# One layer of a gated hybrid encoder: the first norm with tokens on partitions and TensorE transposes, and the memory's norm behind u

## The chip, the core and the metric

The kernel runs on one core of one Trainium2 chip. The core has five engines with queues of their own: TensorE (PE; its weight loads are listed apart as PEld), VectorE (DVE), ScalarE (ACT), GpSimd (POOL) and SyncE (SP), which here only issues DMAs. The metric is the time of one execution in device microseconds. One execution was also recorded by the hardware profiler; its trace and the page made from it are what the prediction reads.

## The reference

The layer works on a residual stream x of 512 tokens by 1024 channels and on 256 memory tokens of the same width, in float32. Cut to what this case touches:

```python
def rmsnorm(x, g):
    r = lax.rsqrt(jnp.mean(xf * xf, axis=-1, keepdims=True) + EPS)
    return (xf * r).astype(x.dtype) * g
...
u = rmsnorm(h, g_mix[l])
proj = u @ w_in[l]            # q, k, v of two attentions, gates, decay columns
...
mkv = rmsnorm(mem, g_mem[l]) @ w_mem_kv[l]
mk, mv = jnp.split(mkv, 2, axis=-1)
```

All that follows hangs on u: a gated linear attention, a forgetting attention ("fox"), an attention into the memory, a gated merge with an output projection, an MLP and a last norm.

## The kernel before

**Products.** Each float32 product is made of three matmuls on numbers that are split into a high and a low part: hi x hi, hi x lo and lo x hi (`mm3`, lines 123 to 125). Weights come in chunks of 128 x 1024 floats (512 KB). For each, ScalarE casts the high part and VectorE subtracts it from the original for the low part (`split_w`, lines 115 and 116; `split`, lines 175 and 176; `lead`, lines 255 and 256, for the first five chunks, which are loaded ahead). `gT` multiplies one chunk of weights (as the stationary operand) with activations that have channels on partitions, 24 matmuls for a chunk. `gN` multiplies four chunks (as the moving operand) with blocks of 128 tokens.

**Order.** TensorE executes its instructions in the order in which the program states them (the manual schedule in `build`). The order on the other engines is made by a scheduler of the language from estimated times; `tc.issue_after` holds instructions back behind a given one. Each engine works through its queue in order.

**The front** (lines 239 to 348) comes first. The memory is loaded with channels on partitions (`memr`), scaled by its gain and split (`mxh`, `mxl`). Because the scale of a token factors out of a product, its norm is not needed for the product itself: the four k projections of the memory (`mk_proj`, chunks 0 to 3 of `w_mem_kv`, 24 matmuls of 256 columns each) and its v projection (`mv`, four more chunks, 48 matmuls of 512 columns) run on the unnormalised memory. ScalarE squares the memory, GpSimd adds the eight squares (`sq_cols`, lines 178 to 188), four one-column matmuls against a column of ones sum over the partitions (`rms_cols`, line 196), VectorE and GpSimd form the power -1/2 (`rsqrt`, lines 202 and 203), and `bcast_rows` (lines 211 to 213) makes from it a diagonal matrix whose product with ones is the scale as a row on all partitions (`rmb`). The v projection is scaled by `rm` when it leaves PSUM.

x is loaded with channels on partitions as well (`xr`). Its squares are added on VectorE and GpSimd, summed by 16 one-column matmuls, spread to rows by four products (`rxb`), and each of the eight slices of 128 channels becomes u by a multiplication with gain and scale (line 339; line 337 on GpSimd for two slices) and is split into `uhi` and `ulo`. TensorE's program is: k projections 0 and 1, the memory's column sums, k projection 2, the memory's broadcast, k projection 3, the v projection with x's column sums behind its second step of three matmuls and x's broadcast behind its seventh.

**Behind the front** TensorE does the G chunk (24 matmuls, the first users of u), the first pair of fox projections fq and fk (`fox_pair(0)`), the decay logs, and then everything else. `mem_split` (behind u by `issue_after`) finishes the memory's k and v: `mk_evac` multiplies each k projection by `rmb` and splits it, and the v projection is split.

Of the kernel before, what the change touches and what calls it, by code (L numbers as in the profile page):

```python
# [17 lines left out]
P = 128  # L18
# [40 lines left out]


@with_exitstack
def hybrid_block(ctx, tc, chunks, wst, xT, memT, xN, cols, gffn, gfin, wup, cst, out):
    nc = tc.nc
    PSUM = bass.MemoryType.PSUM
    index = {c: i for i, c in enumerate(chunks)}
# [3 lines left out]
    def nm(s):  # L69
        uid[0] += 1  # L70
        return f"{s}_{uid[0]}"
# [13 lines left out]
    def at_(shape=None):  # L85
        return pa.tile(shape or [P, 512], F32, tag="a", name=nm("a"))
# [84 lines left out]
    def of(hi, lo):  # L171
        return lambda k, sl: (hi[:, k, sl], lo[:, k, sl])

    def split(hi, lo, src):
        nc.scalar.copy(hi, src)  # L175
        return nc.vector.tensor_tensor(lo, src, f(hi), op=ALU.subtract).ins  # L176

    def sq_cols(pool_, src, n, k, accs, pool_ks, tag):

        e = 1 if k in pool_ks else 0  # L180
        eng = nc.gpsimd if e else nc.vector
        if accs[e] is None:
            accs[e] = pool_.tile([P, n], F32, tag=f"{tag}_acc{e}", name=nm("acc"))
            nc.scalar.activation(accs[e], src[:, k, :], AF.Square)
        else:
            sq = pool_.tile([P, n], F32, tag=f"{tag}_sq{e}", name=nm("sq"), bufs=2)
            nc.scalar.activation(sq, src[:, k, :], AF.Square)
            eng.tensor_tensor(accs[e], accs[e], sq, op=ALU.add)

    def rms_cols(pool_, accs, n):  # L190

        accs = [a for a in accs if a is not None]
        ps = at_()
        for t in range(n // P):
            for i, a in enumerate(accs):
                nc.tensor.matmul(ps[:, t:t + 1], a[:, t * P:(t + 1) * P], ones[:, 0:1], start=i == 0, stop=i == len(accs) - 1)
        return rsqrt(pool_, ps[:, :n // P], 1.0 / D, n // P)

    def rsqrt(pool_, ss, inv, n):
        ms = pool_.tile([P, n], F32, tag="ms", name=nm("ms"), bufs=2)  # L200
        r = pool_.tile([P, n], F32, tag="rr", name=nm("rr"), bufs=2)
        nc.vector.tensor_scalar(ms, ss, inv, EPS, op0=ALU.mult, op1=ALU.add)
        nc.gpsimd.tensor_tensor(r, ms, mhalf[:, :n], op=ALU.pow)
        return r

    def bcast_rows(pool_, r, n, rb):

        ps = at_()
        for t in range(n // P):
            dg = pool_.tile([P, P], F32, tag="dg", name=nm("dg"), bufs=2)  # L210
            nc.scalar.mul(dg, ident, r[:, t:t + 1])
            nc.tensor.matmul(ps[:, t * P:(t + 1) * P], ones, dg, start=True, stop=True)
        nc.scalar.copy(rb, ps[:, :n])
# [24 lines left out]

    with pool("front") as fp:
        rmb = gv[:, 0, 0:M]  # L240
        rxb = fp.tile([P, S], F32, name="rxb")
        memr = fp.tile([P, KT, M], F32, name="memr")
        xr = fp.tile([P, KT, S], F32, name="xr")
        pre = {}

        def lead(key, n, i):
            if key not in pre:
                late = index[key] > 2
                pre[key] = [(fp if late else wp).tile([P, 1024], F32, tag="lead" if late else "raw", name=nm("raw"),
                                                      bufs=2 if late else 3)]  # L250
                pre[key] += [wp.tile([P, 1024], F32R, tag=g, name=nm(g)) for g in ("hi", "lo")]
            sl = slice(i * 1024 // n, (i + 1) * 1024 // n)
            raw, hi, lo = (t[:, sl] for t in pre[key])
            nc.sync.dma_start(raw, wst[index[key]][:, sl])
            nc.scalar.copy(hi, raw)
            nc.vector.tensor_tensor(lo, raw, f(hi), op=ALU.subtract)

        mxh = fp.tile([P, KT, M], F32R, name="mxh")
        mxl = fp.tile([P, KT, M], F32R, name="mxl")
        warm = fp.tile([P, 1], F32, name="warm")  # L260
        nc.vector.memset(warm, 0.0)
        wz = fp.tile([P, 512], BF16, name="wz")
        nc.gpsimd.memset(wz, 0.0)
        ps = at_()
        for _ in range(12):
            nc.tensor.matmul(ps, wz[:, :P], wz, start=True, stop=True)
        nc.scalar.activation(warm, warm, AF.Exp)
        nc.sync.dma_start(cols_s, cols)
        macc, xacc = [None, None], [None, None]
        for j in range(4):  # L270
            nc.sync.dma_start(memr[:, 2 * j:2 * j + 2], memT[:, 2 * j:2 * j + 2])
            for k in (2 * j, 2 * j + 1):
                nc.scalar.mul(mxh[:, k, :], memr[:, k, :], gmem[:, k:k + 1])
                nc.vector.scalar_tensor_tensor(mxl[:, k, :], memr[:, k, :], gmem[:, k:k + 1], f(mxh[:, k, :]),
                                               op0=ALU.mult, op1=ALU.subtract)
                if k == 2 * j:
                    lead(chunks[0], 4, j)
        lead(chunks[1], 1, 0)
        nc.sync.dma_start(cst_s[:, :2 * P], cst[:, :2 * P])
        nc.sync.dma_start(cst_s[:, 6 * P:], cst[:, 6 * P:])  # L280
        lead(chunks[2], 1, 0)
        for j in range(4):
            nc.sync.dma_start(xr[:, 2 * j:2 * j + 2], xT[:, 2 * j:2 * j + 2])
            if j == 1:
                lead(chunks[3], 1, 0)
        lead(chunks[4], 1, 0)
        nc.sync.dma_start(cst_s[:, 2 * P:6 * P], cst[:, 2 * P:6 * P])
        nc.sync.dma_start(wup_s, wup)
        for k in range(KT):
            sq_cols(fp, memr, M, k, macc, range(KT), "m")  # L290

        get_plain = get_w

        def get_first(key):
            return pre[key][1:] if key in pre else get_plain(key)

        get_w = get_first
        UP = (2, 5)

        def mk_evac(h):  # L300
            raw = mk_raw(h)
            nc.vector.tensor_tensor(raw, raw, rmb, op=ALU.mult)
            split(mkh[:, h, :], mkl[:, h, :], raw)

        def mk_raw(h):
            return gkT[h // 2][:, (h % 2) * M:(h % 2) * M + M]

        def mk_proj(h):
            run(gT(("T", "w_mem_kv", P * h), mxh, mxl, lambda ps: nc.scalar.copy(mk_raw(h), ps[:, :M]), n=M))
            for k in (2 * h, 2 * h + 1):  # L310
                sq_cols(fp, xr, S, k, xacc, (1, 2, 3), "x")
                if k in UP:
                    nc.scalar.mul(xr[:, k, :], xr[:, k, :], gmix[:, k:k + 1])

        def mv_evac(t, ps):
            nc.scalar.mul(gqT[t], ps, rm[:, t:t + 1])

        mk_proj(0)
        mk_proj(1)
        rm = rms_cols(fp, macc, M)  # L320
        mk_proj(2)
        bcast_rows(fp, rm, M, rmb)
        mk_proj(3)
        nc.vector.tensor_copy(ident16, ident)
        nc.vector.tensor_scalar(cmask, tri, -1.0, -NEG, op0=ALU.add, op1=ALU.mult)
        nc.vector.tensor_copy(msk_s.rearrange("p a b -> p (a b)"), cst_s[:, 4 * P:6 * P])
        mv = gN([("N", "w_mem_kv", 2 * j, 512) for j in range(4)], of(mxh, mxl), 2, mmt, mv_evac)
        for _ in range(2):
            next(mv)
        rx = rms_cols(fp, xacc, S)  # L330
        for _ in range(5):
            next(mv)
        bcast_rows(fp, rx, S, rxb)
        for k in range(KT):
            ut = fp.tile([P, S], F32, tag="ut", name=nm("ut"), bufs=3)
            if k in UP:
                nc.gpsimd.tensor_tensor(ut, xr[:, k, :], rxb, op=ALU.mult)
            else:
                nc.vector.scalar_tensor_tensor(ut, xr[:, k, :], gmix[:, k:k + 1], rxb, op0=ALU.mult, op1=ALU.mult)
            u_end = split(uhi[:, k, :], ulo[:, k, :], ut)  # L340
        run(mv)
        get_w = get_plain

        def mem_split():
            for h in range(4):
                mk_evac(h)
            for t in range(2):
                split(mvh[:, t, :], mvl[:, t, :], gqT[t])


    with pool("fox") as xp:
# [6 lines left out]
            return gT(("T", "w_in", c), uhi, ulo, evac)  # L358

        run(gT(("G",), uhi, ulo, ga_evac))  # L360
        lf = xp.tile([P, NT, 8], F32, name="lf")
        ab = xp.tile([P, NT, 264], F32, name="ab")
        Fc = xp.tile([P, NT, 8], F32, name="Fc")
# [638 lines left out]
def layout(inputs):  # L1002
# [25 lines left out]
    def tl(a):  # L1028
# [20 lines left out]
    cst[:, 5 * P:6 * P] = same & (s > t)  # L1049
    cst[:, 6 * P:6 * P + 8] = -0.5  # L1050
    arrays = {
        "wst": wst, "xT": tl(x), "memT": tl(mem), "xN": np.ascontiguousarray(x), "cols": cols,
        "gffn": np.ascontiguousarray(np.broadcast_to(np.asarray(inputs["g_ffn"])[0], (P, D))),
        "gfin": np.ascontiguousarray(np.broadcast_to(np.asarray(inputs["g_final"]), (P, D))),
        "wup": wup, "cst": cst,
# [24 lines left out]
```

## Time and profile before

| what | value |
|---|---|
| time, median of 3 runs | 864.08 us (863.69 to 866.55) |
| the profiled execution, its own time | 865.53 us |
| its span in the trace | 863.7 us, mean granted TensorE clock 0.992 |
| busy time of PE / PEld | 847.6 us (98%) / 700.0 us (81%) |
| busy time of DVE / ACT / POOL | 493.8 us (57%) / 403.4 us (47%) / 88.3 us (10%) |
| DMA | 106.10 MB, mean 123 GB/s |

The span runs from the first to the last recorded instruction; the execution's own time is 1.8 us longer. Busy shares are means over the whole span. In rows of single instructions the first number is the start in us from the start of the span, the second the duration, then engine, line, operation, output and inputs, and in brackets the idle time ahead of it with the instruction that ended it; "x24" behind a row says that it stands for 24 instructions of that kind. A wait row gives the summed idle time, its count and its longest. A row of stretches gives a time window, its length, the busy time (and count) of PE, PEld, DVE, ACT and POOL, the clock that TensorE was granted (1.00 is full speed), the mean busy share of the DMA engines and GB/s.

### The profile page before, as it was taken

Reading aid. Unit: us, or ns where it says so; the run is one execution under the profiler, and the core shown is the slowest. Engines: PE = TensorE matmul, PEld = TensorE weight load, DVE = VectorE, ACT = ScalarE, POOL = GpSimd, SP = SyncE. Lnnn points to the kernel's source line nnn. Section 1 sums busy time; section 2 is a strip of 40 time slices with the busy share of each in tenths; the row PEclk is TensorE's granted clock in tenths of the full one; section 3 lists DMA queues with packets and bytes.
Section 4 is the critical chain, followed back from the end, with each engine's and each line's share of the span. In section 5 each row is a group of like instructions: output and inputs, shape, how many; then the busy total and the mean of one; then the engine's idle time right before and its main releaser. Section 6 shows DMA issues by size and latency. Waiting matters only on the chain.

```text
span 863.7 us, 10684 instructions
## 1 busy us (share of the span) xinstructions
PE 847.6 (98%) x4081; PEld 700.0 (81%) x4081; DVE 493.8 (57%) x812; ACT 403.4 (47%) x640; POOL 88.3 (10%) x96
## 2 busy tenths in 40 slices
PE   8999999999999999999999999999999999999995
PEld 5878788888888888787888889888888888888884
DVE  5684556746444546475443446665556645665577
ACT  7665746745243332232333334655455345535642
POOL 5100000000000011212122100011001100110022
PEclk8999999999999999999999999999999999999999
DMA  8333222221221222124332422958625933791156
GB/s 327 123 112 118 91 98 86 90 76 62 92 92 62 90 74 82 41 74 160 109 122 97 146 74 83 352 113 199 204 83 123 278 126 79 145 276 62 25 104 164
DMA packets 31938, 106.10 MB, mean 123 GB/s; under 512 B 3824, under 2 KB 4624, under 8 KB 31888
## 3 DMA queue, kind: packets, MB, share of 16 engines
q1 hardware_dynamic: 24624, 83.92, 27.2%
q0 software_dynamic: 5472, 18.35, 12.0%
q10 hardware_dynamic: 1792, 3.16, 1.0%
q8 instruction: 32, 0.52, 0.3%
q14 instruction: 18, 0.15, 0.1%
HBM read 101.73 MB, written 2.11 MB: 120 GB/s over the span
## 4 chain that ended last, share of the span: by engine, by line
PE 92%; DVE 3%; ACT 1%; DMA 1%; issue 1%; SPq 0%; POOL 0%; DVEq 0%; POOLq 0%; ACTq 0%
PE mm L123 25%; PE mm L124 25%; PE mm L125 25%; PE a L124 3%; PE a L125 3%; PE a L123 3%; PE a L720 1%; PE a L449 1%; DMA h<-G 1%; DMA cst_s<-in_cst_dram 1%; PE a L737 1%; PE a L480 1%; PE a L479 1%; PE a L731 1%; PE a L447 1%
## 5 line engine op out<-in xcount | busy, mean ns | idle before, releaser
L116 DVE TENSOR_TENSOR wlo<-raw,whi 128x1024 fp32r<-128x1024 f32 x104 | 131.1, 1263 | 141.4 <-ACT whi L115 138.4
L115 ACT CAST whi<-raw 128x1024 fp32r<-128x1024 f32 x104 | 109.4, 1053 | 171.5 <-PE mm L124 127.6
L123 PE MATMUL mm<-uhi,whi 128*128 128x512 f32 x360 | 142.4, 396 | 0.0
L124 PE MATMUL mm<-ulo,whi 128*128 128x512 f32 x360 | 140.7, 391 | 1.4 <-DVE ulo L176 1.4
L125 PE MATMUL mm<-uhi,wlo 128*128 128x512 f32 x360 | 140.5, 390 | 0.0
L123 PE MATMUL mm<-u2h,whi 128*128 128x512 f32 x240 | 93.4, 389 | 0.0
L124 PE MATMUL mm<-u2l,whi 128*128 128x512 f32 x240 | 93.4, 389 | 0.0
L125 PE MATMUL mm<-u2h,wlo 128*128 128x512 f32 x240 | 93.4, 389 | 0.0
L124 PEld LDWEIGHTS mm<-ulo,whi 128*128 128x128 f32 x360 | 67.7, 188 | 15.8 <-DVE ulo L176 2.9
L125 PEld LDWEIGHTS mm<-uhi,wlo 128*128 128x128 f32 x360 | 67.6, 188 | 14.5 <-DVE wlo L116 0.4
L176 DVE TENSOR_TENSOR lo<-raw,hi 128x1024 fp32r<-128x1024 f32 x42 | 51.2, 1224 | 48.0 <-ACT hi L175 47.4
L123 PEld LDWEIGHTS mm<-uhi,whi 128*128 128x128 f32 x360 | 67.7, 188 | 13.5 <-issue 0.7
L175 ACT CAST hi<-raw 128x1024 fp32r<-128x1024 f32 x42 | 44.0, 1052 | 61.2 <-PE mm L124 23.5
L960 POOL DMA_DIRECT2D raw<-in_wst_dram x32 | 28.1, 879 | 277.1 <-DVE lo L176 193.6
L124 PEld LDWEIGHTS mm<-u2l,whi 128*128 128x128 f32 x240 | 45.0, 188 | 9.4
L123 PEld LDWEIGHTS mm<-u2h,whi 128*128 128x128 f32 x240 | 45.0, 188 | 9.3
L125 PEld LDWEIGHTS mm<-u2h,wlo 128*128 128x128 f32 x240 | 45.0, 188 | 9.3
L123 PE MATMUL mm<-hi,ch 128*128 128x512 f32 x120 | 46.7, 389 | 0.0
L124 PE MATMUL mm<-lo,ch 128*128 128x512 f32 x120 | 46.7, 389 | 0.0
L125 PE MATMUL mm<-hi,cl 128*128 128x512 f32 x120 | 46.7, 389 | 0.0
L571 POOL TENSOR_TENSOR acc<-acc,th 128x512 f32<-128x512 f32 x16 | 24.1, 1505 | 102.7 <-DVE th L570 102.7
L649 POOL MEMSET qpos<- 64x512 f32 x2 | 1.1, 525 | 269.8 <-PE mm L125 269.7
(316 smaller groups left out, 1646.0 us busy)
## 6 DMA issues: line engine op xcount, KB each, us to landing
raw<-in_wst_dram SPq DMA_DIRECT2D x144, 512.0 KB, 3.3
raw<-in_wst_dram POOLq DMA_DIRECT2D x32, 512.0 KB, 5.3
xr<-in_xT_dram SPq DMA_DIRECT2D x4, 512.0 KB, 8.1
nFb<-dF ACTq DMA_DIRECT2D x8, 256.0 KB, 3.4
h<-in_xN_dram SPq DMA_DIRECT2D x4, 512.0 KB, 7.9
memr<-in_memT_dram SPq DMA_DIRECT2D x4, 256.0 KB, 4.8
h<-G POOLq DMA_DIRECT2D x4, 256.0 KB, 5.7
out_dram<-h ACTq DMA_DIRECT2D x4, 256.0 KB, 2.1
```

Source lines behind the costliest of these rows:

```text
L115: nc.scalar.copy(hi, raw)
L116: nc.vector.tensor_tensor(lo, raw, f(hi), op=ALU.subtract)
L123: nc.tensor.matmul(ps, lh, rh, start=start, stop=False)
L124: nc.tensor.matmul(ps, lh, rl, start=False, stop=False)
L125: nc.tensor.matmul(ps, ll, rh, start=False, stop=stop)
L175: nc.scalar.copy(hi, src)
L176: return nc.vector.tensor_tensor(lo, src, f(hi), op=ALU.subtract).ins
L447: nc.tensor.matmul(ps[:, :w], q, K[e][:, 0, :w], start=True, stop=False)
L449: nc.tensor.matmul(ps[:, :w], q, K[e][:, 1, :w], start=False, stop=True)
L479: nc.tensor.matmul(po[:, q0:], vv, PTh[:, c0:c0 + w], start=n == 0, stop=False)
L571: nc.gpsimd.tensor_tensor(acc[j], acc[j], th, op=ALU.add)
L960: nc.gpsimd.dma_start(raw[to, i], wst[index["B", q, i, x]], accum_op=ALU.add)
```

## The change

x is loaded with tokens on partitions (`xn`, the same array that the kernel reads again later; the same four loads of 512 KB at the same places of SyncE's queue). For each of the four token tiles `x_norm` takes the sum of squares in one ScalarE instruction along the row, the power -1/2 as before, and one VectorE multiplication by the token's scale. One call stands behind each k projection. For each of the eight slices of 128 channels `u_turn` turns four 128 x 128 blocks by TensorE into one PSUM buffer; ScalarE copies it with the gain to `uhi`, VectorE makes `ulo` from the same buffer. The turns stand in TensorE's program behind the fourth step of the v projection, one or two steps of three matmuls between them. Column sums, broadcasts and products for x, the four tiles `xr`, and GpSimd's additions go away.

The memory's squares (two instructions of 128 x 1024) are held back behind the last `uhi` on ScalarE, and three additions on VectorE follow. The rest of its norm (`mem_norm`) stands in TensorE's program between G and fq. The k projections and the v projection wait for it in `mem_split`, where the v projection is now scaled and split at once. Line numbers behind the front shift by two between the two files.

```diff
-    def sq_cols(pool_, src, n, k, accs, pool_ks, tag):
...
-    def rms_cols(pool_, accs, n):
...
-        xr = fp.tile([P, KT, S], F32, name="xr")
+        xn = fp.tile([P, NT, D], F32, name="xn")
+        ssx = small(fp, NT, "ssx")
...
-        for j in range(4):
-            nc.sync.dma_start(xr[:, 2 * j:2 * j + 2], xT[:, 2 * j:2 * j + 2])
-            if j == 1:
+        for t in range(NT):
+            nc.sync.dma_start(xn[:, t, :], xN[t * P:(t + 1) * P, :])
+            if t == 1:
                 lead(chunks[3], 1, 0)
...
-        for k in range(KT):
-            sq_cols(fp, memr, M, k, macc, range(KT), "m")
...
-            for k in (2 * h, 2 * h + 1):
-                sq_cols(fp, xr, S, k, xacc, (1, 2, 3), "x")
-                if k in UP:
-                    nc.scalar.mul(xr[:, k, :], xr[:, k, :], gmix[:, k:k + 1])
-
-        def mv_evac(t, ps):
-            nc.scalar.mul(gqT[t], ps, rm[:, t:t + 1])
-
-        mk_proj(0)
-        mk_proj(1)
-        rm = rms_cols(fp, macc, M)
-        mk_proj(2)
-        bcast_rows(fp, rm, M, rmb)
-        mk_proj(3)
+
+        def x_norm(t):
+
+            sq = fp.tile([P, D], F32, tag="xsq", name=nm("xsq"), bufs=2)
+            nc.scalar.activation(sq, xn[:, t, :], AF.Square, accum_out=ssx[:, t:t + 1])
+            r = rsqrt(fp, ssx[:, t:t + 1], 1.0 / D, 1)
+            nc.vector.tensor_scalar(xn[:, t, :], xn[:, t, :], r, None, op0=ALU.mult)
+
+        def u_turn(k):
+
+            pt = at_()
+            for t in range(NT):
+                nc.tensor.transpose(pt[:, t * P:(t + 1) * P], xn[:, t, k * P:(k + 1) * P], ident)
+            a = nc.scalar.mul(uhi[:, k, :], pt, gmix[:, k:k + 1]).ins
+            return a, nc.vector.scalar_tensor_tensor(ulo[:, k, :], pt, gmix[:, k:k + 1], f(uhi[:, k, :]), op0=ALU.mult,
+                                                  op1=ALU.subtract).ins
+
+        for h in range(4):
+            mk_proj(h)
+            x_norm(h)
+        mv = gN([("N", "w_mem_kv", 2 * j, 512) for j in range(4)], of(mxh, mxl), 2, mmt, lambda t, ps: nc.scalar.copy(gqT[t], ps))
+        for _ in range(4):
+            next(mv)
+        for k in range(KT):
+            u_act, u_end = u_turn(k)
+            for _ in range(1 + k % 2):
+                next(mv)
+        run(mv)
...
-        rx = rms_cols(fp, xacc, S)
-        for _ in range(5):
-            next(mv)
-        bcast_rows(fp, rx, S, rxb)
-        for k in range(KT):
-            ut = fp.tile([P, S], F32, tag="ut", name=nm("ut"), bufs=3)
-            if k in UP:
-                nc.gpsimd.tensor_tensor(ut, xr[:, k, :], rxb, op=ALU.mult)
-            else:
-                nc.vector.scalar_tensor_tensor(ut, xr[:, k, :], gmix[:, k:k + 1], rxb, op0=ALU.mult, op1=ALU.mult)
-            u_end = split(uhi[:, k, :], ulo[:, k, :], ut)
-        run(mv)
         get_w = get_plain
+
+        macc, rm, dg = gv[:, 2, :M], gv[:, 1, :2], gv[:, 3, :M]
+        msq = [fp.tile([P, 4, M], F32, name=f"msq{h}") for h in range(2)]
+        with tc.issue_after(u_act):
+            for h in range(2):
+                nc.scalar.activation(msq[h], memr[:, 4 * h:4 * h + 4, :], AF.Square)
+        nc.vector.tensor_tensor(msq[0], msq[0], msq[1], op=ALU.add)
+        nc.vector.tensor_tensor(msq[0][:, :2, :], msq[0][:, :2, :], msq[0][:, 2:, :], op=ALU.add)
+        nc.vector.tensor_tensor(macc, msq[0][:, 0, :], msq[0][:, 1, :], op=ALU.add)
+
+        def mem_norm():
+
+            ps = at_()
+            for t in range(2):
+                nc.tensor.matmul(ps[:, t:t + 1], macc[:, t * P:(t + 1) * P], ones[:, 0:1], start=True, stop=True)
+            nc.vector.tensor_scalar(rm, ps[:, :2], 1.0 / D, EPS, op0=ALU.mult, op1=ALU.add)
+            nc.gpsimd.tensor_tensor(rm, rm, mhalf[:, :2], op=ALU.pow)
+            pb = at_()
+            for t in range(2):
+                sl = slice(t * P, (t + 1) * P)
+                nc.scalar.mul(dg[:, sl], ident, rm[:, t:t + 1])
+                nc.tensor.matmul(pb[:, sl], ones, dg[:, sl], start=True, stop=True)
+            nc.scalar.copy(rmb, pb[:, :M])
 
         def mem_split():
             for h in range(4):
                 mk_evac(h)
             for t in range(2):
-                split(mvh[:, t, :], mvl[:, t, :], gqT[t])
+                nc.scalar.mul(mvh[:, t, :], gqT[t], rm[:, t:t + 1])
+                nc.vector.scalar_tensor_tensor(mvl[:, t, :], gqT[t], rm[:, t:t + 1], f(mvh[:, t, :]), op0=ALU.mult,
+                                               op1=ALU.subtract)
...
         run(gT(("G",), uhi, ulo, ga_evac))
+        mem_norm()
```

More of the change, by code (lines that the diff above doesn't have):

```diff
@@ L61, in hybrid_block @@
 @with_exitstack
-def hybrid_block(ctx, tc, chunks, wst, xT, memT, xN, cols, gffn, gfin, wup, cst, out):
+def hybrid_block(ctx, tc, chunks, wst, memT, xN, cols, gffn, gfin, wup, cst, out):
     nc = tc.nc
@@ L176, in split @@
         return nc.vector.tensor_tensor(lo, src, f(hi), op=ALU.subtract).ins
-    def sq_cols(pool_, src, n, k, accs, pool_ks, tag):
[L180 to L184, printed above, removed]
-        else:
-            sq = pool_.tile([P, n], F32, tag=f"{tag}_sq{e}", name=nm("sq"), bufs=2)
-            nc.scalar.activation(sq, src[:, k, :], AF.Square)
-            eng.tensor_tensor(accs[e], accs[e], sq, op=ALU.add)
-    def rms_cols(pool_, accs, n):
[L192 to L197, printed above, removed]
     def rsqrt(pool_, ss, inv, n):
@@ L240, in hybrid_block @@
         rmb = gv[:, 0, 0:M]
-        rxb = fp.tile([P, S], F32, name="rxb")
         memr = fp.tile([P, KT, M], F32, name="memr")
-        xr = fp.tile([P, KT, S], F32, name="xr")
+        xn = fp.tile([P, NT, D], F32, name="xn")
+        ssx = small(fp, NT, "ssx")
         pre = {}
@@ L268, in hybrid_block @@
         nc.sync.dma_start(cols_s, cols)
-        macc, xacc = [None, None], [None, None]
         for j in range(4):
@@ L297, in hybrid_block @@
         get_w = get_first
-        UP = (2, 5)
         def mk_evac(h):
@@ L326, in hybrid_block @@
         nc.vector.tensor_copy(msk_s.rearrange("p a b -> p (a b)"), cst_s[:, 4 * P:6 * P])
-        mv = gN([("N", "w_mem_kv", 2 * j, 512) for j in range(4)], of(mxh, mxl), 2, mmt, mv_evac)
-        for _ in range(2):
-            next(mv)
-        rx = rms_cols(fp, xacc, S)
-        for _ in range(5):
-            next(mv)
-        bcast_rows(fp, rx, S, rxb)
-        for k in range(KT):
-            ut = fp.tile([P, S], F32, tag="ut", name=nm("ut"), bufs=3)
-            if k in UP:
-                nc.gpsimd.tensor_tensor(ut, xr[:, k, :], rxb, op=ALU.mult)
-            else:
-                nc.vector.scalar_tensor_tensor(ut, xr[:, k, :], gmix[:, k:k + 1], rxb, op0=ALU.mult, op1=ALU.mult)
-            u_end = split(uhi[:, k, :], ulo[:, k, :], ut)
-        run(mv)
-        get_w = get_plain
+        get_w = get_plain
+        macc, rm, dg = gv[:, 2, :M], gv[:, 1, :2], gv[:, 3, :M]
[18 more added lines that the diff above has]
+            nc.scalar.copy(rmb, pb[:, :M])
         def mem_split():
@@ L1051, in layout @@
     arrays = {
-        "wst": wst, "xT": tl(x), "memT": tl(mem), "xN": np.ascontiguousarray(x), "cols": cols,
+        "wst": wst, "memT": tl(mem), "xN": np.ascontiguousarray(x), "cols": cols,
         "gffn": np.ascontiguousarray(np.broadcast_to(np.asarray(inputs["g_ffn"])[0], (P, D))),
```

## The prediction

> **What bounds the kernel now.** I read the page first: its span, and the chain of work that ended last.
>
> ```profile
> span 863.7 us, 10684 instructions
> PE 92%; DVE 3%; ACT 1%; DMA 1%; issue 1%; SPq 0%; POOL 0%; DVEq 0%; POOLq 0%; ACTq 0%
> ```
>
> TensorE carries nine tenths of the chain. Next the waits of TensorE alone, first before 62 us and then after it.
>
> ```profile
> PE mm L124 <- DVE ulo L176: 1.4, 3, 0.8
> ```
>
> ```profile
> PE a L463 <- DVE Pt L456: 0.2, 1, 0.2
> ```
>
> The second row is the only wait of TensorE from 62 us to the end, so a microsecond won or lost before 62 us arrives at the end unchanged. The diff touches only the front (lines 239 to 348) and one call behind the G chunk. Behind that the instruction order of the engines is the same in both kernels, but for a few ScalarE steps of the decay logs. So the whole effect is the time at which TensorE reaches the fq chunk. Its rows, from the memory's value projection (mv) on:
>
> ```profile
> 27.27 0.50 PE L124 MATMUL mm<-lo,mxh 128*128 128x512 f32 x1 [0.70 <-DVE lo L256]
> ...
> 28.53 1.84 PE L196 MATMUL a<-cst_s,acc 128*128 128x1 f32 x16
> 30.23 0.71 PE L123 MATMUL mm<-hi,mxh 128*128 128x512 f32 x1
> 30.74 0.63 PE L124 MATMUL mm<-lo,mxh 128*128 128x512 f32 x1
> 31.17 0.63 PE L125 MATMUL mm<-hi,mxl 128*128 128x512 f32 x1
> ...
> 35.35 0.60 PE L212 MATMUL a<-dg,cst_s 128*128 128x128 f32 x4
> ...
> 36.76 0.48 PE L123 MATMUL mm<-whi,mxh 128*128 128x512 f32 x1
> ...
> 42.31 0.39 PE L123 MATMUL mm<-whi,mxh 128*128 128x512 f32 x1
> ...
> 42.99 0.39 PE L123 MATMUL mm<-uhi,whi 128*128 128x512 f32 x1
> ...
> 50.77 0.39 PE L123 MATMUL mm<-uhi,whi 128*128 128x512 f32 x1
> ```
>
> The matmul at 27.27 is mv's second, 42.99 the first of G, 50.77 the first of fq. From 42.31 to 42.99 three matmuls take 0.68, so one of 512 columns costs 0.228 us; from 30.74 to 31.17 one costs 0.43. That is the clock: the stretches of 3.41 us below give the busy time of TensorE, its count, and the granted clock (PEclk).
>
> ```profile
> 6.35:9.76 3.41, 2.56 (x15) 1.94 (x14) 3.32 (x7) 3.30 (x11) 1.97 (x3) 1.00 1.05 352
> 9.76:13.17 3.41, 1.88 (x13) 1.47 (x13) 3.33 (x6) 3.41 (x8) 2.14 (x4) 1.00 1.04 415
> 13.17:16.58 3.41, 2.79 (x14) 2.50 (x13) 2.62 (x2) 3.41 (x8) 3.33 (x3) 0.51 1.02 408
> 26.83:30.24 3.41, 2.97 (x22) 2.76 (x22) 3.26 (x4) 1.82 (x2) 0.00 (x0) 1.00 0.11 28
> 30.24:33.65 3.41, 3.41 (x10) 2.72 (x10) 0.16 (x1) 1.23 (x3) 1.03 (x1) 0.51 0.78 264
> ```
>
> A stretch with 1.88 us busy is followed by half clock, one with 2.56 is not. The stretch from 26.83 is nearly busy, but 16 of its 22 instructions stream one column each, and half clock follows too. A half-clock stretch of 3.41 us costs about 8 x (0.43 - 0.228) = 1.6 us.
>
> **The change, part by part.**
>
> *The start.* The squares of the memory leave ScalarE's and GpSimd's queues. GpSimd's additions ran beside VectorE's splits:
>
> ```profile
> 10.77 1.04 ACT L255 CAST hi<-raw 128x1024 fp32r<-128x1024 f32 x1
> ...
> 12.03 3.76 DVE L256 TENSOR_TENSOR lo<-raw,hi 128x256 fp32r<-128x256 f32 x3
> ...
> 12.26 5.37 POOL L188 TENSOR_TENSOR acc<-acc,sq 128x256 f32<-128x256 f32 x4 [0.44 <-ACT sq L187]
> ...
> 14.17 0.58 PE L125 MATMUL mm<-mxh,lo 128*128 128x256 f32 x1 [0.62 <-DVE lo L256]
> ```
>
> ```profile
> L116 DVE TENSOR_TENSOR wlo<-raw,whi 128x1024 fp32r<-128x1024 f32 x104 | 131.1, 1263 | 141.4 <-ACT whi L115 138.4
> ```
>
> A 1024-wide split usually takes 1.26. It can now begin when its cast ends, 11.8, and end at 13.05, so the second k projection goes on 1.1 us earlier than at 14.17. The memory's column sums (L196, between these rows) go from here:
>
> ```profile
> 18.82 0.41 PE L125 MATMUL mm<-mxh,lo 128*128 128x256 f32 x1
> 19.04 0.85 PE L196 MATMUL a<-cst_s,acc 128*128 128x1 f32 x4
> 19.74 0.51 PE L123 MATMUL mm<-mxh,hi 128*128 128x256 f32 x1
> ```
>
> ```profile
> 20.00:22.80 2.80, 2.80 (x24) 2.80 (x25) 1.94 (x3) 2.33 (x5) 2.64 (x2) 0.99 1.03 409
> ```
>
> One of 256 columns costs 2.80/24 = 0.117 at full clock, some 0.21 at half. In the changed kernel 9.76 to 13.17 is still thin, so half clock begins at 13.2. But the stretch after it is now full, so I end half clock at 16.6 instead of 20.0. Of the 46 matmuls left of projections two and three, 16 run at half clock, 30 x 0.117 = 3.5 follow: the third ends near 20.1 (before: 19.74 + 24 x 0.117 with a slow first, about 22.8). If half clock lasts two stretches again, it ends near 21.6. I take 20.1.
>
> *The start of mv gives most of that back.* In ScalarE's new order the squares of x tiles 2 and 3 stand behind the copy of the third k projection, and the cast of mv's first chunk behind them. On VectorE its split stands behind both tiles' scaling. The tiles themselves are in time, as their loads keep place and size:
>
> ```profile
> L283 SPq DMA_DIRECT2D xr<-in_xT_dram x4: 328/380/437, 7.9 to 10.7; - x4
> ...
> DMA to landing us min/median/max: 5.7/8.1/8.1
> ```
>
> The last lands by 10.7 + 8.1 = 18.8. Prices of the rest:
>
> ```profile
> L777 ACT ACTIVATE hsq<-h 128x512 f32<-128x512 f32 x8 | 5.0, 630 | 10.5 <-DVE h L800 10.5
> ...
> L777 ACT ACTIVATION_READ_ACCUMULATOR hsq<-h 128x1 f32 x8 | 1.5, 188 | 0.0
> ```
>
> ```profile
> L456 DVE TENSOR_SCALAR Pt<-Pt,ri 128x512 f32<-128x512 f32 x8 | 3.9, 484 | 0.2
> ```
>
> ```profile
> 19.92 0.16 DVE L202 TENSOR_SCALAR ms<-a 128x2 f32<-128x2 f32 x1 [4.13 <-PE a L196]
> ...
> 20.16 0.72 POOL L203 TENSOR_TENSOR rr<-ms,cst_s 128x2 f32<-128x2 f32 x1 [2.53 <-DVE ms L202]
> ...
> 20.91 0.70 ACT L211 ACTIVATE dg<-cst_s,rr 128x128 f32<-128x128 f32 x2 [0.31 <-POOL rr L203]
> ```
>
> A square of 1024 is not in the trace: at least 0.63, at most 2 x 0.63; I take 1.05, the duration of the cast of that width, plus 0.19 for its sum. Scaling 1024 wide lies between 0.48 and 0.97; I take 0.8. Then: copy ends 20.5, two squares 22.9, cast 23.9; on VectorE, mean and power of the last tile end 22.9 + 1.0 = 23.9, scaling 24.7, the two small mask instructions about 25.1, the split 26.4. So mv's second matmul starts near 26.4, 0.9 before 27.27, while TensorE has finished the fourth k projection at 20.1 + 2.8 = 22.9 and waits some 3.3 us. Bounds: 25.3 with the lower prices, 28 with two half-clock stretches at the start.
>
> *From there to the end of G.* Gone are x's column sums (30.23 - 28.53 = 1.70), the four broadcast products (36.76 - 35.35 = 1.41), and the stalls of G, which takes 7.78 instead of 24 x 0.228 = 5.47. New are 32 transposes. The nearest rows are those of u2:
>
> ```profile
> 518.41 1.04 PE L829 MATMUL a<-cst_s,un 128*128 128x128 f32 x8
> 519.20 0.48 PE L123 MATMUL mm<-fhi,mh 128*128 128x512 f32 x1
> 519.51 0.40 PE L124 MATMUL mm<-flo,mh 128*128 128x512 f32 x1
> ```
>
> Eight take 0.79, and the matmul behind them 0.31 instead of 0.23. Eight groups of four are 8 x (0.40 + 0.08) = 3.8. Their evacuations (a scaled copy and a subtraction for each u tile, instead of three steps) run beside the 36 mv matmuls left; the fifth group waits for the first buffer's subtraction, which I put 3 us earlier. So 71 matmuls at 0.228 (16.2), 3.8, and one half-clock stretch after the 3.3 us hole (1.6): 21.6, where before took 50.77 - 27.27 = 23.5. G ends near 48.0, 2.7 us ahead.
>
> *The memory's norm behind G takes this.* Its column sums, power, diagonal and broadcast stand in TensorE's order ahead of fq with nothing between. Priced by the rows above: sums 0.45, latency 0.25, from the mean to the first diagonal 20.91 - 19.92 = 1.0, two diagonals 0.7, the last products 0.3: 2.7. fq starts near 50.7, level with 50.77. The squares and additions that feed the sums finish beside G, by my walk 0.8 us ahead of its end; if later, it costs one for one. Within this hole TensorE streams next to nothing for about 2.3 us, so I let a half-clock stretch follow: +1.6.
>
> Sum: -0.9 + (21.6 - 23.5) + 2.7 + 1.6 = +1.5 on the profiled execution's 865.53 (span 863.73 and 1.8 around it): 867.0. That execution stands 1.45 above the median of 864.08, about one half-clock stretch, and the runs shown spread by 2.9. The new holes are long enough to be met whatever the phase, so I do not give the 1.45 back.
>
> **The rivals.**
>
> *Not slower: the holes do not halve the clock.* The point is a stretch between 1.88 and 2.56 us busy. The mv hole (3.3 us) cut in the middle leaves 1.75 on each side, the norm's leaves 2.2. If the norm's hole trips nothing: 865.4. If neither does: 863.8. For it: the second is borderline; against: the stretch from 9.76. [...]
>
> *Half clock lasts longer.* The stretch from 13.17 was 2.79 busy and did not end it. If transposes count as idle, a mv stretch is only some 75% busy and half clock stays for one or two stretches more: 868.6 to 870.2. [...] The trace has eight at 518.41 between matmuls that stay at 0.23, which does not test a release.
>
> *The change does what it says and u's path sets the end.* If mv hides the squares better than I walk (lower bounds, 25.3), and G's 2.3 us of stalls go with no stretch tripped, 861 to 862.5.
>
> **How the numbers follow.** Forecast 867.0, chance 0.40; norm's hole free 0.20; neither trips 0.11; longer half clock 0.22; u's path 0.07. No change is within 0.3% (2.6 us, about what a measurement of this kernel can tell): 861.5 to 866.7. The forecast stands just above this window and neither-trips inside it, so each is split by its own spread: 0.29 of the forecast's 0.40 counts as slower and 0.11 as same; of neither-trips' 0.11, 0.06 counts as same and 0.05 as faster. Slower: 0.29 and 0.22, 0.51. Same: 0.11, 0.20 and 0.06, 0.37. Faster: 0.05 and 0.07, 0.12. The range leaves out the ends of the last two: 862.8 to 869.8.
>
> **What would show it.** mv's second matmul waiting for its split until 26 to 27, the wait over 2.5 us; G with no wait; a wait of TensorE for the diagonal of about 1.7 at 48 to 51; granted clock 0.5 behind each of the two; the same distance from fq to the end. A mv hole under 1 us, or the column sums late, would prove me wrong.

## The result and the profile after

The changed kernel takes 866.38 us (median of 20 runs, 864.24 to 869.13) against 863.52 for the kernel before beside it (20 runs, 861.39 to 867.5): a ratio of 1.0033, 95% interval 1.0020 to 1.0046. It is slower by 2.9 us, or 0.33%: just above the 0.3% below which the prediction speaks of no change, and the interval reaches a little below that. Its profiled execution took 868.43 us, 2.9 more than that of before; each of the two lies 2.0 above the median of its kernel.

The page of the changed kernel: TensorE is still nearly all of the chain, only over a longer span.

```profile
span 866.7 us, 10674 instructions
PE 91%; ACT 3%; DVE 2%; DMA 1%; issue 1%; SPq 0%; POOL 0%; DVEq 0%; POOLq 0%; ACTq 0%
```

Three of the waits of TensorE before 62 us (in total, count, longest):

```profile
PE mm L123 <- ACT hi L234: 2.5, 4, 1.2
PE mm L124 <- DVE lo L235: 2.2, 1, 2.2
PE a L336 <- ACT gv L335: 1.5, 1, 1.5
```

and the first of two after it:

```profile
PE mm L123 <- DVE K L176: 0.5, 1, 0.5
```

G's wait for the low part of u (1.4 before) is gone, as is every wait inside G. In its place stand the wait for the v projection's first split (L124, 2.2), that for the memory's diagonal (L336, 1.5), and, which I had not priced, 0.5 for the second K. The first row belongs to the casts of the chunks that are loaded ahead, 0.62 of it to the v projection's first; before, TensorE waited 3.0 us in all for their low parts. TensorE's own rows, at the places of those shown of before:

```profile
24.89 0.50 PE L123 MATMUL mm<-hi,mxh 128*128 128x512 f32 x1 [0.62 <-ACT hi L234]
27.59 0.49 PE L124 MATMUL mm<-lo,mxh 128*128 128x512 f32 x1 [2.20 <-DVE lo L235]
...
31.80 0.60 PE L295 MATMUL a<-cst_s,xn 128*128 128x128 f32 x4
...
43.64 0.40 PE L123 MATMUL mm<-uhi,whi 128*128 128x512 f32 x1
...
49.10 0.50 PE L329 MATMUL a<-cst_s,gv 128*128 128x1 f32 x4
51.07 0.78 PE L336 MATMUL a<-gv,cst_s 128*128 128x128 f32 x4 [1.47 <-ACT gv L335]
51.61 0.47 PE L123 MATMUL mm<-uhi,whi 128*128 128x512 f32 x1
```

G runs from 43.64 to 49.10 without a stall (5.46 for 24 matmuls; 7.78 before). fq starts at 51.61, 0.84 later than before. From there the distance is no longer the same. The decay logs start at

```profile
64.20 1.94 PE L369 MATMUL a<-wup_s,gaT 128*128 128x264 f32 x8
```

in the changed kernel and at

```profile
61.91 1.94 PE L371 MATMUL a<-wup_s,gaT 128*128 128x264 f32 x8
```

in the one before. That is 12.59 against 11.14 behind the start of fq, 1.45 more for the same 48 matmuls. Stretches of the changed kernel (length, busy PE, PEld, DVE, ACT, POOL with counts, clock, DMA share, GB/s) show why:

```profile
26.83:30.24 3.41, 2.65 (x7) 2.11 (x8) 2.98 (x3) 0.17 (x1) 0.00 (x0) 0.70 0.13 31
30.24:33.65 3.41, 3.41 (x18) 2.79 (x17) 0.56 (x1) 1.65 (x3) 0.00 (x0) 0.80 0.75 275
...
50.70:54.10 3.40, 3.03 (x11) 2.50 (x12) 3.21 (x7) 2.36 (x6) 0.00 (x0) 0.70 0.52 172
54.10:57.50 3.40, 3.40 (x14) 2.73 (x13) 2.05 (x7) 1.15 (x4) 0.00 (x0) 0.80 0.00 1
```

Behind each of the two holes the mean clock is 0.70 and 0.80 in two neighbouring stretches. They lie across one stretch at 0.5: the deficits of 0.30 and 0.20 add up to one half, and in finer stretches the clock is 0.50 from 28.20 to 31.55 and from 52.10 to 55.40. So the kernel after pays: start of the v projection +0.32 (27.59 for 27.27), to the end of G -2.0 (21.5 for 23.5, with one stretch at half clock in each: before it stands behind x's column sums, 0.50 from 30.40 to 33.60, now behind the first hole), hole +2.5, half clock +1.45, wait for K +0.5. That is +2.8 of the 3.0 between the spans.

### The profile page after: what moved, and what is told of

Read it like the earlier page. It is cut to its first block, busy times and chain, and to the rows that moved or that the text cites. A ratio compares the mean times of both kernels' runs of the same rounds, so it can differ in the third digit from the quotient of the medians.

```text
span 866.7 us, 10674 instructions
## 1 busy us (share of the span) xinstructions
PE 848.5 (98%) x4089; PEld 701.9 (81%) x4089; DVE 488.4 (56%) x812; ACT 401.1 (46%) x627; POOL 75.2 (9%) x88
## 4 chain that ended last, share of the span: by engine, by line
PE 91%; ACT 3%; DVE 2%; DMA 1%; issue 1%; SPq 0%; POOL 0%; DVEq 0%; POOLq 0%; ACTq 0%
PE mm L123 25%; PE mm L124 25%; PE mm L125 25%; PE a L124 3%; PE a L123 3%; PE a L125 3%; PE a L718 1%; DMA raw<-in_wst_dram 1%; DMA h<-G 1%; PE a L447 1%; PE a L735 1%; PE a L478 1%; PE a L477 1%; PE a L729 1%; PE a L445 1%
## 5 line engine op out<-in xcount | busy, mean ns | idle before, releaser
L124 PE MATMUL mm<-ulo,whi 128*128 128x512 f32 x360 | 140.9, 391 | 0.0
L124 PE MATMUL mm<-u2l,whi 128*128 128x512 f32 x240 | 93.4, 389 | 0.0
L124 PEld LDWEIGHTS mm<-ulo,whi 128*128 128x128 f32 x360 | 68.1, 189 | 13.1
L124 PEld LDWEIGHTS mm<-u2l,whi 128*128 128x128 f32 x240 | 45.0, 188 | 9.3
L124 PE MATMUL mm<-lo,ch 128*128 128x512 f32 x120 | 46.7, 389 | 0.0
L176 DVE TENSOR_TENSOR cl<-ss,ch 128x1024 fp32r<-128x1024 f32 x16 | 19.6, 1225 | 13.4 <-ACT ch L175 13.4
```

The lines of the kernel that those rows point to most:

```text
L124: nc.tensor.matmul(ps, lh, rl, start=False, stop=False)
```

## The experiments

Theory A: the change saves time in u, and gives it back in the two holes, by their idle time and by half clock behind them. Rivals: the transposes cost it (B), the clock has nothing to do with the holes (C, F), the work is only moved (D, E, G). All ratios are to the kernel before on the same chip, with 95% intervals.

**Each half alone: x_part and mem_part.** x_part keeps the memory's norm of before; mem_part keeps x as before, and its squares share the buffers of the leading chunks.

x_part, against the changed kernel:

```diff
 ...
 mk_proj(0); x_norm(0); mk_proj(1)
+rm = rms_cols(fp, macc, M)
 x_norm(1); mk_proj(2)
+bcast_rows(fp, rm, M, rmb)
 x_norm(2); mk_proj(3); x_norm(3)
...
-mem_norm()
```

mem_part, against the kernel before:

```diff
-rm = rms_cols(fp, macc, M)
-bcast_rows(fp, rm, M, rmb)
...
 run(gT(("G",), uhi, ulo, ga_evac))
+mem_norm()
```

> Only the x half of the change: x token-major, normalised and turned as in the changed kernel; the memory's squares, GpSimd additions, column sums and broadcast as in the kernel before. Theory A (the memory norm's hole behind G and the half-clock stretch after it cost 2.5 + 1.6 us, the x half is worth something): G runs into fq without a hole, the memory's sums and broadcast come back (about 1.3 us on TensorE) and the low split of the second k chunk is late again (1.1): faster than the changed kernel's 866.4 by 2 to 3, so 863 to 864.5. Rival B (the transposes, 3.5 to 4 us on TensorE, are what costs): 866 or more, and mem_part alone would be the fast one.

> Only the memory half: x column-wise as in the kernel before; the memory's squares behind u, its norm between G and fq. Theory A: gains about 1.3 us of sums and broadcast and up to 1.1 at the second k projection, pays 2.5 for the hole, 1.6 for half clock behind it: before plus 1.5 to 2.5, 865 to 866. Rival B: the hole is paid by what went from the front, 861 to 863.5.

x_part: 861.6 us, 0.9982 (0.9970 to 0.9994). mem_part: 875.79, 1.0145 (1.0121 to 1.0169). Rival B falls: with all 32 transposes the kernel is faster than before by 1.4 us at its median. Both sizes were missed. x_part is 4.8 us faster than the changed kernel, where A had 2 to 3: in its profile, which is of its fastest run, the clock is 1.00 all through the front (3.4 to 61.4 us), and the wait for the v projection's first split is 1.3 instead of 2.2. So the memory half costs some 4.8 us when it is added to the x half; alone it loses 12.8, where I expected 1.5 to 2.5. TensorE in mem_part, behind G:

```profile
53.55 1.02 PE L350 MATMUL a<-cst_s,gv 128*128 128x1 f32 x4 [4.88 <-DVE gv L344]
56.04 1.23 PE L357 MATMUL a<-gv,cst_s 128*128 128x128 f32 x4 [1.47 <-ACT gv L356]
```

and VectorE just ahead:

```profile
46.43 1.46 DVE L333 TENSOR_TENSOR ulo<-ut,uhi 128x512 fp32r<-128x512 f32 x2
47.81 2.35 DVE L116 TENSOR_TENSOR wlo<-raw,whi 128x1024 fp32r<-128x1024 f32 x2
50.08 1.22 DVE L342 TENSOR_TENSOR msq<-msq,msq 128x1024 f32<-128x1024 f32 x1
51.22 1.22 DVE L116 TENSOR_TENSOR wlo<-raw,whi 128x1024 fp32r<-128x1024 f32 x1
...
53.07 0.43 DVE L344 TENSOR_TENSOR gv<-msq 128x256 f32<-128x256 f32 x1
```

With x made as before, VectorE is at u until 47.9. The squares' additions queue behind it and behind three weight splits, and TensorE stands for 4.88 and 1.47. In the changed kernel, where u is finished earlier, the last addition ends at 48.5, 0.6 ahead of the end of G:

```profile
48.12 0.42 DVE L323 TENSOR_TENSOR gv<-msq 128x256 f32<-128x256 f32 x1
```

**The memory's norm out of the hole: norm_in_fq; and for mem_part, mem_in_fq.** The same instructions, with products of fq (and fk) between them.

```diff
 def mem_norm():
     ...
     nc.gpsimd.tensor_tensor(rm, rm, mhalf[:, :2], op=ALU.pow)
+    yield
     pb = at_()
 ...
-mem_norm()
 ...
 with tc.issue_after(u_end):
-    next(pair)
+    for n in (2, 5):          # mem_in_fq: (8, 5)
+        run(islice(pair, n))
+        next(norm)
     mem_split()
```

> The changed kernel, but the memory's sums stand behind the second step of fq and its broadcast behind the seventh, so TensorE has 15 matmuls (3.4 us) to run while the power and the diagonal are made. Theory A: the 2.5 us hole leaves about 1.0 of real work (sums, broadcast), and no half clock behind it: 866.4 - 1.5 - 1.6 = 863.3, 862.5 to 864. Rival C (idle time moves, the clock does not hang on the hole): only 1.5 us, 865. Rival D (mem_split's VectorE and ScalarE work comes later and delays q or k's evacuation and the decay logs): 866 or more, with a new wait of TensorE between 60 and 75 us.

> The memory half alone, with its sums behind all of fq and its broadcast behind the fifth step of fk. Theory A (its 875.8 came from the wait for the squares and additions, which VectorE did late because u was late, and from half clock behind that hole): the wait of 4.9 us, the 1.5 for the diagonal and most of the half clock go, 862 to 865. Rival G (the order of the whole front is disturbed, k projections and u too): 868 or more.

norm_in_fq: 862.1 us, 0.9990 (0.9978 to 1.0002), 4.3 less than the changed kernel. That is more than A's 3.1, just outside its 862.5 to 864, and C's 865 and D's 866 fall. In its profile the clock is 1.00 from 45 to 62 us, and the wait of 0.5 for the second K, which A did not count, is absent. TensorE waits for neither sums nor diagonal:

```profile
47.97 0.50 PE L329 MATMUL a<-cst_s,gv 128*128 128x1 f32 x4
...
51.88 0.60 PE L337 MATMUL a<-gv,cst_s 128*128 128x128 f32 x4
```

mem_in_fq: 866.6 us, 1.0040 (1.0021 to 1.0058). Moving the norm takes away 9.2 of the nearly 13 that mem_part loses, and about 3.7 over the kernel before remain: 866.6 lies neither in A's 862 to 865 nor at G's 868 or more. Its trace still has G's waits for the low part of u (1.4, as before the change) and 1.75 ahead of the v projection's first two products (0.70 before), and its runs spread from 863.64 to 868.96. What makes up the 3.7 stays open.

**The first hole: cast_first.** The squares and scalings of x tiles 2 and 3 go behind the cast of the v projection's first chunk.

```diff
-lead(chunks[4], 1, 0)
+mv_hi, mv_lo = lead(chunks[4], 1, 0)      # lead returns its cast and its split
 ...
 for h in range(4):
     mk_proj(h)
-    x_norm(h)
+    if h < 2: x_norm(h)
+with tc.issue_after(mv_hi), tc.issue_after(mv_lo):
+    for t in (2, 3): x_norm(t)
```

> The changed kernel, but the squares and scalings of x tiles 2 and 3 stand behind the cast and split of the v projection's first chunk. Theory A: the v projection's second matmul starts near 24.5 us instead of 27.6; the first transposes then wait for tile 3 until about 28.5, a hole of about 1.5 instead of 2.8, so 3 us less before the first transpose if no half clock follows, 1.5 if it does: 863.4 to 865. Rival E (the first transposes are the true limit, whatever stands ahead): the wait moves whole to the transposes, 866.

862.34 us, 0.9990 (0.9977 to 1.0003): 4 less than the changed kernel, more than A's 1.5 to 3 (its profile shows what may be a part of the rest, further down), and E falls. In the changed kernel ScalarE had both squares ahead of the cast, and VectorE a scaling ahead of the split (ScalarE at 21.70 to 23.80, VectorE at 25.31 and 26.32):

```profile
21.70 1.07 ACT L287 ACTIVATE xsq<-xn 128x1024 f32<-128x1024 f32 x1
...
22.75 1.05 ACT L287 ACTIVATE xsq<-xn 128x1024 f32<-128x1024 f32 x1
...
23.80 1.04 ACT L234 CAST hi<-raw 128x1024 fp32r<-128x1024 f32 x1
...
25.31 0.76 DVE L289 TENSOR_SCALAR xn<-xn,rr 128x1024 f32<-128x1024 f32 x1 [0.73 <-POOL rr L182]
...
26.32 1.22 DVE L235 TENSOR_TENSOR lo<-raw,hi 128x1024 fp32r<-128x1024 f32 x1
```

In cast_first the same places of TensorE are

```profile
22.52 0.50 PE L124 MATMUL mm<-lo,mxh 128*128 128x512 f32 x1 [0.28 <-DVE ms L181]
26.49 0.33 PE L294 MATMUL a<-cst_s,xn 128*128 128x128 f32 x1 [0.84 <-DVE xn L288]
```

so 2.8 of waiting became 1.1: 0.28 for the split (it ends at 22.47; the row names the small instruction behind it in VectorE's queue), and 0.84 of the transposes for the last tile.

**The clock by itself: fill_both, fill_norm, again.** Products that nobody reads are put into the holes; nothing is taken away. `again` is the changed kernel on the chip of fill_both.

```diff
+pf = at_()
+for _ in range(24):                       # fill_both only, ahead of the v projection
+    nc.tensor.matmul(pf[:, :M], mxh[:, 0, :P], mxh[:, 0, :], start=True, stop=True)
 ...
 nc.gpsimd.tensor_tensor(rm, rm, mhalf[:, :2], op=ALU.pow)
+pf = at_()
+for _ in range(6):                        # fill_both and fill_norm
+    nc.tensor.matmul(pf, uhi[:, 0, :P], uhi[:, 0, :], start=True, stop=True)
```

> The changed kernel with products that nobody reads put into its two holes: 24 of 256 columns ahead of the v projection, 6 of 512 columns between the memory's sums and its broadcast; nothing else moves. Theory A (part of a hole's price is the half clock after it, in the executions in which it trips): TensorE reaches fq no earlier, but the stretches at clock 0.5 behind the two places are gone: 863.5 to 865.5, highest run below 867.5. Rival F (the holes cost their idle time and nothing else, the half clock comes from elsewhere): 866 to 867, as without filling.

> The changed kernel itself on the same chip as the three above: 866.4, 865.5 to 867, with runs that lie in separate groups between 864 and 869.

> The changed kernel with 6 products of 512 columns that nobody reads between the memory's sums and its broadcast, and nothing at the v projection. Theory A: the half clock behind G goes, that behind the v projection's hole stays: between the changed kernel's 866 and the 863.3 with both holes filled, 864 to 865.5. If it equals 863.3, the hole behind G has the whole effect; if 866, the v projection's has.

again: 865.98 us, 1.0032 (1.0021 to 1.0042). fill_both: 863.26, 1.0002 (0.9992 to 1.0012). fill_norm, in a later comparison: 864.65, 1.0018 (1.0004 to 1.0033). Thirty useless products make the kernel 2.7 us faster, so F falls. The mean clock of the runs is 0.993 to 0.997 in fill_both and 0.989 to 0.994 in again. With only the hole behind G filled the time lies between, as A expected; by their intervals fill_norm is not quite apart from again, nor from fill_both. fill_both's profile behind its two places:

```profile
26.83:30.24 3.41, 3.20 (x17) 2.48 (x16) 3.33 (x3) 0.52 (x1) 0.00 (x0) 1.00 0.09 14
...
50.70:54.10 3.40, 3.40 (x16) 2.78 (x15) 3.37 (x9) 2.30 (x7) 0.00 (x0) 1.00 0.46 154
```

This profiled execution is still the slowest of fill_both's twelve, 865.63: at its start it has two stretches at half clock (0.50 from 13.17 to 16.58), which the products don't touch. So a part of the spread comes from ahead of the holes. The changed kernel's own profile has them too and took 868.43, 2.8 more.

In again, by contrast, both places slow down:

```profile
23.40:26.80 3.40, 1.83 (x7) 1.47 (x8) 3.40 (x6) 1.10 (x2) 0.00 (x0) 0.89 0.14 51
26.83:30.24 3.41, 3.41 (x13) 2.75 (x12) 0.36 (x2) 1.08 (x2) 0.00 (x0) 0.61 0.87 265
...
50.70:54.10 3.40, 3.40 (x11) 2.69 (x10) 2.88 (x9) 1.41 (x4) 0.00 (x0) 0.60 0.20 77
```

**The better versions: both, x_cast.** norm_in_fq and cast_first together; and x_part with the order of cast_first.

> norm_in_fq and cast_first together in the changed kernel: the memory's sums and broadcast spread through fq, and the squares and scalings of x tiles 2 and 3 behind the cast of the v projection's first chunk. Theory A (two separate holes): the gains add, 866.4 - 4.3 - 4.0 = 858; 857.5 to 860. Rival E (one limit shared, such as u's own evacuations): about the better of the two, 861.5 to 862.5.

> x_part (x token-major, the memory's norm as in the kernel before) with the cast_first order. Theory A: x_part waited 1.3 us for the v projection's first split; with the cast first about 1 us less, 860 to 861. If it ends above both, the memory half of the change is worth having once its norm makes no hole; if below, it isn't.

both: 859.54 us, 0.9959 (0.9944 to 0.9974). x_cast: 860.54, 0.9972 (0.9961 to 0.9983). The two cures add, with some 1.5 us short of the plain sum (858), and `both` beats the kernel before by 3.7 us and the changed one, on the same chip, by 6.4. Rival E falls here too. That the memory half of the change is worth its 1.0 us over x_cast is not shown; the intervals overlap.

## Why the prediction was right

**Direction and size were right:** 867.0 forecast, 866.38 measured, and slower was the likeliest of the three signs. The path was right as well: time is won where x's sums and broadcast and G's stalls go, and given back in two holes and at half clock behind them. That the number came so close is luck. The sum made +1.5 where the profiled pair differs by 2.9, because two terms were wrong; and it stood on a profiled execution of before that took 2.0 more than the 863.52 now measured. The two errors nearly cancel.

- *The start of the v projection* was mis-sized: -0.9 forecast (26.4), +0.32 measured (27.59). The order of the queues was as said, and the wait nearly (0.62 and 2.20 for 3.3). What failed is "the third ends near 20.1": the half clock lasted two stretches, from about 11.2 (a product of 0.52) to 18.0 (0.28 again), and the third k projection ended only at 21.4, where ScalarE copies it. The prediction had named this case ("near 21.6", with 28 for the v projection) and not taken it:

```profile
11.19 0.52 PE L123 MATMUL mm<-mxh,hi 128*128 128x256 f32 x1
...
18.00 0.28 PE L123 MATMUL mm<-mxh,hi 128*128 128x256 f32 x1
...
21.43 0.37 ACT L282 COPY gkT<-mm 128x256 f32<-128x256 f32 x1 [1.56 <-PE mm L125]
```

  In again no half clock came there at all (two stretches, then TensorE's rows):

```profile
9.76:13.17 3.41, 2.44 (x14) 1.82 (x14) 2.62 (x6) 2.81 (x5) 0.00 (x0) 1.00 1.04 392
13.17:16.58 3.41, 3.41 (x30) 3.41 (x31) 2.20 (x4) 3.07 (x7) 0.61 (x2) 1.00 1.03 416
...
24.97 0.50 PE L124 MATMUL mm<-lo,mxh 128*128 128x512 f32 x1 [2.21 <-DVE lo L235]
...
46.52 0.50 PE L329 MATMUL a<-cst_s,gv 128*128 128x1 f32 x4
```

  The same program reached the same matmul at 24.97, 2.6 sooner.
- *From there to the end of G*: 21.6 forecast, 21.5 measured, and 21.55 in again (24.97 to 46.52). The transposes cost what the rows of u2 gave: 0.36 for a group of four (0.40 forecast) and 0.08 on the product behind it.
- *The norm's hole*: 2.7 forecast, 2.51 measured. *Half clock behind it*: 1.6 forecast, 1.45 measured.
- *Not in the sum*: 0.5 for the second K. I named the moved ScalarE steps of the decay logs and priced them at nothing. ScalarE before, and in the changed kernel:

```profile
66.40 0.58 ACT L175 CAST K<-mm 64x512 fp32r<-64x512 f32 x1
67.01 1.09 ACT L375 ACTIVATE ab<-ab 128x1056 f32<-128x1056 f32 x1
```

```profile
67.09 1.09 ACT L373 ACTIVATE ab<-ab 128x1056 f32<-128x1056 f32 x1
...
69.27 0.58 ACT L175 CAST K<-mm 64x512 fp32r<-64x512 f32 x1
```

  The scheduler put the exponential (1.09) ahead of the second K's cast, the split on VectorE follows that cast, and TensorE had to wait for it (the row of 0.5 above). In norm_in_fq and both the wait is absent; in x_part, whose memory norm is that of before, it is there, so it is not a price of the hole behind G. With it and the half clock, "the same distance from fq to the end" did not hold: 815.1 us against 812.9.
- *"The new holes are long enough to be met whatever the phase" is wrong.* In fill_norm's profile the v projection's hole, the same 2.21, was followed by clock 1.00:

```profile
23.40:26.80 3.40, 1.73 (x8) 1.42 (x9) 3.40 (x6) 1.22 (x2) 0.00 (x0) 1.00 0.14 52
26.83:30.24 3.41, 3.41 (x21) 2.85 (x20) 1.71 (x3) 2.26 (x3) 0.00 (x0) 1.00 0.83 250
```

  The hole behind G can go free as well. In cast_first it is the same 1.47, and the clock behind it was 1.00, which may be a part of that kernel's larger gain:

```profile
45.48 0.78 PE L339 MATMUL a<-gv,cst_s 128*128 128x128 f32 x4 [1.47 <-ACT gv L338]
```

```profile
45.60:49.00 3.40, 3.40 (x17) 2.88 (x18) 3.21 (x8) 2.35 (x7) 0.00 (x0) 1.00 0.42 154
```

  So the half clock is a chance at each hole, and the median holds its mean price. fill_both puts that at 2.7 us for both holes together, where I had 1.6 at each in full. How large the chance is, one profile for each kernel doesn't show. The rival "neither trips" was one end of what the executions do, not a kernel of its own.

Half clock came at other places in other executions, two of one program among them. It began near 13.2 in the profile of before (0.51 in the stretch from 13.17), near 11.2 in that of the changed kernel (0.50 from 11.15 to 17.90), and not before 26 in again, which is the same program (1.00 from 9.76 to 23.40, 0.89 in the stretch from 23.40). I had read the places of one execution as if they were the program's.

## What to carry to other kernels

Follow what stands behind a moved instruction in every queue: here the squares of x ahead of one cast on ScalarE, and a chain through VectorE, GpSimd and ScalarE between two products on TensorE, cost more than the change saved, and reordering alone gave 6.4 us back. A chain through other engines belongs beside products that don't need it, split into its issue and its use (norm_in_fq: 4.3 us). And price a hole on TensorE at its idle time plus a chance of a half-clock stretch behind it (here 2.5 and, where it came, 1.45 us behind G), from several executions rather than one.

## What the runs showed of the hardware

A hole of 1.5 us of waiting (2.0 from the first sum to the diagonal's products, 49.10 to 51.07) was followed by a half-clock stretch of about 3.4 us in the changed kernel (0.50 from 52.10 to 55.40) and in again (0.89 and 0.60 in the stretches from 47.30 and 50.70); in cast_first the same hole was followed by none (1.00 in the stretch from 45.60). So holes of 1.5 and 2.2 us of waiting cost more than their length in some executions, and filling both with useless products paid 2.7 us (863.26 for 865.98). In the changed kernel's trace, groups of four transposes among products ran without a loss of clock: it is 1.00 from 34.13 to 47.79, with six groups in it, and the four from 31.80 take 0.36, the products behind them 0.31 and then 0.23:

```profile
32.16 0.48 PE L123 MATMUL mm<-whi,mxh 128*128 128x512 f32 x1
32.47 0.39 PE L124 MATMUL mm<-wlo,mxh 128*128 128x512 f32 x1
32.70 0.39 PE L125 MATMUL mm<-whi,mxl 128*128 128x512 f32 x1
```

Whether transposes delay the return of the full clock is hardly tested. In again only one group stands in a stretch at half clock (0.61 on the mean from 26.83 to 30.24); it takes 0.65, and the products behind it are at full speed (the next starts at 29.56, the one after it 0.32 later):

```profile
28.91 0.89 PE L295 MATMUL a<-cst_s,xn 128*128 128x128 f32 x4
```
